# Four mixer steps traced later, and the branch sum moved from GpSimd to VectorE, in a hybrid decoder layer

## The chip, the cores and the metric

The kernel runs on one core of a Trainium2 chip. A core has TensorE (PE: matrix multiplies, with weight loads listed as PEld), VectorE (DVE), ScalarE (ACT), GpSimd (POOL) and SyncE (SP), each with an instruction queue that is worked off in order, and DMA engines that move data between HBM and the on-chip memories. The metric is the device time of one execution in microseconds. Before the change it is 2330.97 us, the median of three runs (2327.71, 2330.97 and 2331.9 us).

## The reference: what is computed

One layer on 256 tokens of width 2048, all float32. Cut to what matters:

```python
x = x + 0.5 * swiglu(rms_norm(x), ffn1...)            # d_ff 5632
h = rms_norm(x); p = h @ w_in                          # 1024 + 2*256 + 3360 + 4096 columns
q, k, v, p_rwkv, gates = split(p)
y_attn = sliding_window_attention(q, k, v, sinks)      # 16 heads of 64, 4 kv heads, blocks of 128
y_rwkv = rwkv7_time_mix(p_rwkv, ...)                   # recurrence over 256 steps, 16 heads of 64
gate_attn, gate_rwkv = split(sigmoid(gates))
merged = gate_attn * (y_attn @ w_proj_attn) + gate_rwkv * (y_rwkv @ w_proj_rwkv)
x = x + merged @ w_out
x = x + cross_attention(x, mem)
x = x + 0.5 * swiglu(rms_norm(x), ffn2...)
out = rms_norm(x)
```

The line `merged = ...` is the sum of the two branches. In the time mix, the decay and the rate `a` are sigmoids of small matrix products, and everything after them (keys, the inverse of a triangular system, the state) hangs on them.

## The kernel before, in words

**Products.** Nearly all TensorE time goes into products of the 256 tokens with weight matrices. A weight block arrives in units of 256 rows by up to 512 columns (`KU = 2` chunks of 128 rows). ScalarE rounds a unit to `hi` (line 299) and VectorE computes the rest `lo = raw - hi` (line 300). The activations are held as `hi` and `lo` too, and for each chunk and each half of the tokens `multiply` issues three matmuls of 512 columns: `xh*hi`, `xh*lo`, `xl*hi` (lines 336 to 338). These are called the large matmuls below; a unit has 12 of them. `next_unit` requests loads four units ahead on SP's queue and divides units two ahead (`LOADED`, `AHEAD`). `hi`, `lo` and `raw` have 3, 3 and 4 buffers. A product fills two PSUM banks (`acc`, of three); ScalarE or VectorE reads them at its end.

**Background steps.** Everything else in the mixer is written as Python generators, sorted into groups (`Interleave`). After each `multiply`, that is every six large matmuls, `tick` advances the first one, two or three generators of each group by one step, up to their next `yield`. So a `yield` places the following instructions six large matmuls later in the traced program; `idle(n)` is n yields. A planner that knows instruction costs then fixes each engine's final order, close to the traced order but not equal to it. On the chip each engine follows that order strictly: when an instruction's operand is late, all behind it on that engine wait.

**The steps the change touches**, in the order in which they run:
- `keys_values` (line 515): copies the keys into `kd` by ScalarE (line 521), mirrors them onto the other 64 partitions by two DMAs from GpSimd's queue (line 522), copies the values, idles, and then lets attention begin (`bg.seen.add("kv")`).
- `attend` (line 533), eight times, two at a time: scores (PE, line 542), scale and mask (DVE, line 548), row maximum (line 555), exponentials (ACT, line 567), normalization (DVE, lines 572 to 575), one yield, transposes of the probabilities (PE, line 581), copies (ACT, line 584), weighted values (PE, line 589).
- `decay_and_rate` (line 644): four groups of small matmuls (PE, line 661) into PSUM banks tagged `mm` (three of them, two per group), four sigmoids after each (ACT, line 668), one yield between the groups; then scans (DVE, line 675) and exponentials. It is the first of the serial group `ew`: `removal_keys` (lines 717 and 754), `substitute` (lines 775 to 789), `receptances` and `values` (lines 835 and 843) come behind it. The `pair` chains of the recurrence (lines 902 to 970) follow `values`, and `finish` (lines 995 to 1015) makes `yr` from them.
- the last part: four products of `yr` with `w_proj_rwkv`. At the end of each, VectorE multiplies by the gate (`gl`, line 1055), GpSimd adds the other branch (`ml`, line 1056), and `merged` transposes the sum on PE (line 347, tile `ml`) and splits it into `mt` (lines 352 and 353), which the product with `w_out` reads.

Of the kernel before, what the change touches and what calls it, by code (L numbers as in the profile page):

```python
# [120 lines left out]
def decoder_layer(ctx: ExitStack, tc: tile.TileContext, a: dict, out: bass.AP):  # L121
# [357 lines left out]
    with tc.tile_pool(name="mx", bufs=1, reuse_waits="tile") as sp:  # L479
# [35 lines left out]
        def keys_values():  # L515

            b = feat(tok_kv, C4[:2])
            v = kd[:].rearrange("p (c e) t -> p c e t", e=2)
            for e in range(2):
                r, o = slice(64 * e, 64 * e + 64), slice(64 - 64 * e, 128 - 64 * e)  # L520
                act.copy(v[r, :, e, :], b[r])
                pool.dma_start(v[o, :, e, :], v[r, :, e, :])
            yield
            for t in range(2):
                dve.tensor_copy(vt[:, t, :], tok_kv[:, t, KV_W : 2 * KV_W])
            yield from idle(2)
            bg.seen.add("kv")

        bg.spawn("feat", keys_values())
# [3 lines left out]
        def attend(kv, qb):  # L533
            yield from wait_for("kv")
            w = P * (qb + 1)
            tq = slice(qb * P, qb * P + P)
            s = t4("s", (P, 2, 2, T))
            b = [mm() for _ in range(2)]
            for c in range(2):
                for e in range(2):  # L540
                    r = slice(64 * e, 64 * e + 64)
                    pe.matmul(  # L542
                        b[e][:, c * w : (c + 1) * w], qt[kv // 2][r, 2 * (kv % 2) + c, tq],
                        kd[r, kv, :w], start=True, stop=True,
                    )
            bias = abias[:, 1 - qb :, :].rearrange("p a b -> p (a b)")
            for e in range(2):
                dve.scalar_tensor_tensor(
                    s[:, e, :, :w], b[e][:, : 2 * w].rearrange("p (c w) -> p c w", c=2), 0.125,
                    bias.unsqueeze(1).to_broadcast([P, 2, w]), ALU.mult, ALU.add,  # L550
                )
            yield
            s3 = s[:].rearrange("p e c w -> p (e c) w")
            m = stat.tile([P, 4], F32, tag="m", name="m")
            dve.tensor_reduce(m[:], s3[:, :, :w], AX.X, ALU.max)
            sk = sink4[:, kv]
            m22 = m[:].rearrange("p (e c) -> p e c", e=2)
            dve.tensor_tensor(m22, m22, sk, ALU.max)
            nm = stat.tile([P, 4], F32, tag="nm", name="nm")
            dve.tensor_scalar(nm[:], m[:], -1.0, None, ALU.mult)  # L560
            es = stat.tile([P, 4], F32, tag="es", name="es")
            dve.tensor_tensor(es[:].rearrange("p (e c) -> p e c", e=2), sk, m22, ALU.subtract)
            yield
            den = stat.tile([P, 4], F32, tag="den", name="den")
            act.activation(es[:], es[:], AF.Exp)
            for i in range(4):
                act.activation(
                    s3[:, i, :w], s3[:, i, :w], AF.Exp, bias=nm[:, i : i + 1],
                    accum_out=den[:, i : i + 1],
                )  # L570
            yield
            dve.tensor_tensor(den[:], den[:], es[:], ALU.add)
            dve.reciprocal(den[:], den[:])
            for i in range(4):
                dve.tensor_scalar(s3[:, i, :w], s3[:, i, :w], den[:, i : i + 1], None, ALU.mult)
            yield
            pt = t4("pt", (P, 2, 4, P))
            for kb in range(qb + 1):
                b = tr()
                for i in range(4):  # L580
                    pe.transpose(  # L581
                        b[:, i * P : (i + 1) * P], s3[:, i, kb * P : (kb + 1) * P], ident[:]
                    )
                act.copy(pt[:, kb], b[:].rearrange("p (i q) -> p i q", i=4))
            yield
            b = tr()
            for kb in range(qb + 1):
                for e in range(2):
                    pe.matmul(  # L589
                        b[64 * e : 64 * e + 64, : 2 * P], vt[:, kb, kv * 64 : kv * 64 + 64],  # L590
                        pt[:, kb, 2 * e : 2 * e + 2, :].rearrange("p c q -> p (c q)"),
                        start=kb == 0, stop=kb == qb,
                    )
            b3 = b[:, : 2 * P].rearrange("p (c q) -> p c q", c=2)
            hi, lo = (ya.at(p, 2 * kv, 2)[:, :, tq] for p in range(2))
            act.copy(hi, b3)
            dve.tensor_tensor(lo, b3, f32(hi), ALU.subtract)
            if qb:
                ya.done |= {2 * kv, 2 * kv + 1}
            if kv == 3 and qb:  # L600
                bg.seen.add("attn")
# [42 lines left out]
        def decay_and_rate():  # L644
            yield from wait_for("small")
            yield from wait_for("attn")
            wa = t4("wa", (P, RW))
            pool.dma_start(wa[0:64, :], W["rwkv_w2"])
            pool.dma_start(wa[64:128, :], W["rwkv_a2"])
            act.activation(xwa[0:64, :], xwa[0:64, :], AF.Tanh)  # L650
            act.activation(xg, xg, AF.Sigmoid)
            yield
            for h in range(2):
                cs.append(t4("cs"))
                aa.append(t4("aa"))
                for q in (0, 2):
                    b = [mm() for _ in range(2)]
                    for i in range(2):
                        for e in range(2):
                            r, c = slice(64 * e, 64 * e + 64), (4 * h + q + i) * P  # L660
                            pe.matmul(
                                b[e][:, i * T : (i + 1) * T], wa[r, c : c + P], xwa[r, :],
                                start=True, stop=True,
                            )
                    for i in range(2):
                        for e, (dst, bias) in enumerate(((cs[h], w0), (aa[h], a0))):
                            c = 4 * h + q + i
                            act.activation(
                                dst[:, q + i, :], b[e][:, i * T : (i + 1) * T], AF.Sigmoid,
                                bias=bias[:, c : c + 1],  # L670
                            )
                    yield
            for h in range(2):
                for c in range(4):
                    dve.tensor_tensor_scan(
                        cs[h][:, c, :], keep2, cs[h][:, c, :], 0.0, ALU.mult, ALU.add
                    )
                    if c % 2:
                        yield
                c3 = halves(cs[h])  # L680
                mid = stat.tile([P, 8], F32, tag="mid", name="mid")
                dve.tensor_copy(mid[:], c3[:, :, 63])
                dve.tensor_tensor(
                    c3, c3, mid[:].unsqueeze(2).to_broadcast([P, 8, P]), ALU.subtract
                )
                dec.append(stat.tile([P, 4], F32, tag="dec", name="dec"))
                dve.tensor_tensor(dec[h][:], cs[h][:, :, 127], mid[:, 1:8:2], ALU.add)
                yield
                act.activation(dec[h][:], dec[h][:], AF.Exp, scale=-DECAY)

                ee.append(t4("ee", (P, 8, P)))
                e0.append(stat.tile([P, 8], F32, tag="e0", name="e0"))
                act.activation(e0[h][:], mid[:], AF.Exp, scale=DECAY)
                act.activation(ee[h][:], c3, AF.Exp, scale=-DECAY)
                yield
                act.activation(cs[h][:], cs[h][:], AF.Exp, scale=DECAY)
                yield
            bg.seen.add("decay")
# [342 lines left out]
        mt = act_tiles("mt", 4)  # L1041

        def merged(m, n):
            yield
            for q in (0, 2):
                split(mt, 4 * n + q, 2, feat(m, C4[q : q + 2]))
                yield

        for n in range(4):
            g, m = t4("gl", (P, 2, 512)), t4("ml", (P, 2, 512))  # L1050
            pool.dma_start(g[:], blk(grd, n))
            pool.dma_start(m[:], blk(md, n))
            pr = product(yr, W["w_proj_rwkv"])
            for t in range(2):
                dve.tensor_tensor(g[:, t, :], pr[t][:], g[:, t, :], ALU.mult)
                pool.tensor_tensor(m[:, t, :], g[:, t, :], m[:, t, :], ALU.add)  # L1056
            bg.spawn("feat", merged(m, n))

        n3 = Norm(g_cross)
# [164 lines left out]
```

## Time and profile before

| | before |
|---|---|
| median of 3 runs | 2330.97 us (2327.71 to 2331.9) |
| the profiled execution | 2332.38 us, span 2330.7 us, mean granted TensorE clock 0.998 |
| PE busy | 2307.1 us (99%) |
| DVE, ACT, POOL busy | 1258.9 us (54%), 1078.9 us (46%), 130.3 us (6%) |
| HBM traffic | 185 GB/s over the span |
| the mixer's products | from about 748 us to about 1490 us of the span |

In the profile, times are counted from the span's start. A timeline row gives start, duration, engine, line, operation, tiles and shape, and how many instructions it merges; square brackets give the idle time of that engine just before, and what ended it. In a row of waits stand the total waited, how often, and the longest. PE is busy nearly all the time, so a change in another engine's work matters only where PE waits for that engine, or where the granted clock changes.

### The profile page before, as it was taken

To read this page: it belongs to the slowest core of one execution; us is meant where nothing else is said; L and a number is where in the kernel's file an instruction comes from. 1 tells how busy PE (TensorE), PEld (TensorE's weight loads), DVE (VectorE), ACT (ScalarE), POOL (GpSimd) and SP (SyncE) were. 2 spreads that over 40 slices of the span, in tenths; PEclk is the share of its full clock that TensorE was granted. 3 is DMA by queue.
4 is the path that set the end of the run, shared out by engine and by line. 5 is a ranking of instruction groups with operands and counts; after the bars stand their busy time and mean duration, and the time that the engine had idled before them with its cause. 6 is when DMAs were issued, how large, how long until landed. Compare 5 with 4: busy or idle time off the path is not lost.

```text
span 2330.7 us, 27378 instructions
## 1 busy us (share of the span) xinstructions
PE 2307.1 (99%) x10869; PEld 1898.4 (81%) x10869; DVE 1258.9 (54%) x1395; ACT 1078.9 (46%) x1425; POOL 130.3 (6%) x192
## 2 busy tenths in 40 slices
PE   8999999999999999999999999999999999999998
PEld 6888888888888877888888878888888888888887
DVE  4545544544556477795444556546545544544545
ACT  5443344434445477444344446555444344434444
POOL 1000000000000000200220030001000000000001
PEclk9999999999999999999999999999999999999999
DMA  8555655555554544666432576548555555555553
GB/s 284 187 189 191 197 184 197 182 198 192 187 188 153 172 129 140 196 229 212 123 96 94 165 247 216 201 158 298 187 192 187 193 196 184 198 182 197 191 189 127
DMA packets 219857, 432.71 MB, mean 186 GB/s; under 512 B 14268, under 2 KB 17041, under 8 KB 219729
## 3 DMA queue, kind: packets, MB, share of 16 engines
q1 hardware_dynamic: 211520, 405.58, 52.5%
q0 software_dynamic: 8176, 25.38, 3.4%
q8 instruction: 85, 1.39, 0.2%
q14 instruction: 44, 0.35, 0.0%
q10 hardware_dynamic: 32, 0.01, 0.0%
HBM read 417.56 MB, written 13.11 MB: 185 GB/s over the span
## 4 chain that ended last, share of the span: by engine, by line
PE 93%; issue 4%; DVE 1%; ACT 1%; POOL 1%; DMA 0%; SPq 0%; POOLq 0%; ACTq 0%
PE acc L336 28%; PE acc L337 28%; PE acc L338 28%; PE tr L347 2%; PE mm L934 1%; PE tr L902 1%; POOL ml L1056 0%; PE mm L542 0%; ACT hi L299 0%; PE tr L917 0%; DMA x<-in_x_dram 0%; PE tr L921 0%; PE tr L581 0%; PE tr L1004 0%; PE tr L589 0%
## 5 line engine op out<-in xcount | busy, mean ns | idle before, releaser
L300 DVE TENSOR_TENSOR lo<-raw,hi 128x1024 fp32r<-128x1024 f32 (+1 forms) x769 | 941.8, 1225 | 962.2 <-ACT hi L299 961.7
L299 ACT CAST hi<-raw 128x1024 fp32r<-128x1024 f32 (+1 forms) x769 | 805.6, 1048 | 1063.8 <-PE acc L338 1026.5
L336 PE MATMUL acc<-hi,xhi 128*128 128x512 f32 (+1 forms) x2016 | 799.2, 397 | 0.0
L337 PE MATMUL acc<-lo,xhi 128*128 128x512 f32 (+1 forms) x2016 | 786.0, 390 | 0.0
L338 PE MATMUL acc<-hi,xlo 128*128 128x512 f32 (+1 forms) x2016 | 785.4, 390 | 0.0
L336 PEld LDWEIGHTS acc<-hi,xhi 128*128 128x128 f32 x2016 | 379.9, 188 | 79.9 <-issue 3.6
L338 PEld LDWEIGHTS acc<-hi,xlo 128*128 128x128 f32 x2016 | 379.4, 188 | 79.8 <-issue 1.3
L337 PEld LDWEIGHTS acc<-lo,xhi 128*128 128x128 f32 x2016 | 380.0, 188 | 78.1 <-issue 3.3
L336 PE MATMUL acc<-hi,hhi 128*128 128x512 f32 x704 | 275.5, 391 | 0.0
L338 PE MATMUL acc<-hi,hlo 128*128 128x512 f32 x704 | 274.2, 389 | 0.0
L337 PE MATMUL acc<-lo,hhi 128*128 128x512 f32 x704 | 274.0, 389 | 0.0
L338 PEld LDWEIGHTS acc<-hi,hlo 128*128 128x128 f32 x704 | 132.1, 188 | 27.6
L337 PEld LDWEIGHTS acc<-lo,hhi 128*128 128x128 f32 x704 | 132.2, 188 | 27.1
L336 PEld LDWEIGHTS acc<-hi,hhi 128*128 128x128 f32 x704 | 132.2, 188 | 26.9
L336 PE MATMUL acc<-hi,mthi 128*128 128x512 f32 x128 | 51.2, 400 | 0.0
L338 PE MATMUL acc<-hi,mtlo 128*128 128x512 f32 x128 | 50.2, 392 | 0.0
L337 PE MATMUL acc<-lo,mthi 128*128 128x512 f32 x128 | 49.9, 390 | 0.0
L1177 POOL TENSOR_TENSOR x<-x,fin 128x512 f32<-128x512 f32 x6 | 8.9, 1507 | 695.3 <-ACT junk L1175 695.3
L470 POOL DMA_DIRECT2D x1d<-x x4 | 3.0, 745 | 710.4 <-DVE x L427 710.4
L415 ACT ACTIVATE hb<-acc,rs 128x512 f32<-128x512 f32 x44 | 30.2, 690 | 19.5 <-PE acc L338 19.5
L352 ACT CAST hhi<-tr 128x512 fp32r<-128x512 f32 x44 | 25.7, 584 | 16.3 <-PE tr L347 16.3
L373 ACT ACTIVATE xhi<-tr,gains 128x256 fp32r<-128x256 f32 x48 | 22.0, 471 | 22.0 <-DVE xlo L374 16.1
(289 smaller groups left out, 1641.3 us busy)
## 6 DMA issues: line engine op xcount, KB each, us to landing
raw<-in_ffn_w_up_dram SPq DMA_DIRECT2D x88, 1024.0 KB, 5.1
raw<-in_ffn_w_down_dram SPq DMA_DIRECT2D x88, 1024.0 KB, 5.0
raw<-in_ffn_w_gate_dram SPq DMA_DIRECT2D x86, 1024.0 KB, 5.1
raw<-in_w_in_dram SPq DMA_DIRECT2D x136, 512.0 KB, 3.5
raw<-in_w_out_dram SPq DMA_DIRECT2D x32, 512.0 KB, 4.3
raw<-in_w_proj_attn_dram SPq DMA_DIRECT2D x16, 512.0 KB, 3.7
raw<-in_w_proj_rwkv_dram SPq DMA_DIRECT2D x16, 512.0 KB, 5.0
raw<-in_w_cross_kv_dram SPq DMA_DIRECT2D x16, 512.0 KB, 3.5
```

What stands on the lines that cost most here:

```text
L299: act.copy(hi[:, s], raw[:, s])
L300: dve.tensor_tensor(lo[:, s], raw[:, s], f32(hi[:, s]), ALU.subtract)
L336: pe.matmul(o, xh, hi[:, i, :], start=k + i == 0, stop=False)
L337: pe.matmul(o, xh, lo[:, i, :], start=False, stop=False)
L338: pe.matmul(o, xl, hi[:, i, :], start=False, stop=k + i == nk - 1)
L347: pe.transpose(b[:, o : o + P], tok[:, t, col : col + P], ident[:])
L352: act.copy(x.at(0, c, n), src)
L373: last = act.activation(self.x.at(0, c), b[:, j, :], AF.Copy, scale=g)
L415: act.activation(hb[:, t, :], pg[t][:], AF.Silu, scale=norm.r[t])
L902: pe.matmul(b[e][:, m * P : (m + 1) * P], x1[r, j, cs_], x2[r, j, cs_], start=True, stop=True,)
L934: pe.matmul(vb[:, (o + e) * P : (o + e + 1) * P], lhs(e), rhs[:], start=first and e == 0, stop=True, **ek,)
L1177: pool.tensor_tensor(xs, xs, fin[:, n * 512 : (n + 1) * 512], ALU.mult)
```

## The change

Four background steps get more yields, and one addition changes its engine:

```diff
@@ keys_values
-            yield from idle(2)
+            yield from idle(4)
             bg.seen.add("kv")
@@ attend, between normalization and transposes
-            yield
+            yield from idle(2)
             pt = t4("pt", (P, 2, 4, P))
@@ decay_and_rate, after each of the four groups of sigmoids
-                    yield
+                    yield from idle(2)
@@ merged
         def merged(m, n):
-            yield
+            yield from idle(4)
@@ after each product of yr with w_proj_rwkv
                 dve.tensor_tensor(g[:, t, :], pr[t][:], g[:, t, :], ALU.mult)
-                pool.tensor_tensor(m[:, t, :], g[:, t, :], m[:, t, :], ALU.add)
+                dve.tensor_tensor(m[:, t, :], g[:, t, :], m[:, t, :], ALU.add)
```

Attention starts two ticks later and each attend takes one tick more; each decay group comes one tick later than it did; the transposes of the summed branches come three ticks later. No instruction is added to the program text, and none is removed. As the planner orders the changed program, ScalarE gets two more loads of an activation table.

## The prediction

> **What bounds the kernel now.** I read the page's busy shares and the chain that ended last, then PE's own waits, then the stretches and moments around those waits.
>
> ```profile
> PE 2307.1 (99%) x10869; PEld 1898.4 (81%) x10869; DVE 1258.9 (54%) x1395; ACT 1078.9 (46%) x1425; POOL 130.3 (6%) x192
> PE 93%; issue 4%; DVE 1%; ACT 1%; POOL 1%; DMA 0%; SPq 0%; POOLq 0%; ACTq 0%
> ```
>
> PE is the bound: 99% busy and 93% of the chain. The change removes no PE work, so only two things can move the time: moments at which PE waits for another engine, and the clock it is granted. PE's waits in the mixer:
>
> ```profile
> PE tr L347 <- POOL ml L1056: 3.1, 3, 1.0
> PE mm L542 <- DMA kd<-kd: 1.1, 1, 1.1
> PE tr L581 <- DVE s L575: 0.6, 1, 0.6
> PE mm L661 <- ACT aa L668: 0.5, 1, 0.5
> PE mm L661 <- ACT cs L668: 0.3, 1, 0.3
> ```
>
> Columns: total us, times, longest. These five rows add up to 5.6 us, and they are just the places where the change puts yields. That is most of what moving steps can win; the rest is the clock.
>
> **1. The branch sum.** The second of the four products of yr, from its end at 1367.6:
>
> ```profile
> 1367.32 1.28 DVE L1055 TENSOR_TENSOR gl<-acc,gl 128x512 f32<-128x512 f32 x2
> 1368.10 3.50 POOL L1056 TENSOR_TENSOR ml<-gl,ml 128x512 f32<-128x512 f32 x2 [8.20 <-DVE gl L1055]
> 1368.90 1.57 DVE L300 TENSOR_TENSOR lo<-raw,hi 128x1024 fp32r<-128x1024 f32 x1 [0.30 <-ACT hi L299]
> 1370.34 0.27 PE L347 MATMUL tr<-ident,ml 128*128 128x128 f32 x1
> 1371.65 0.55 PE L347 MATMUL tr<-ident,ml 128*128 128x128 f32 x3 [1.04 <-POOL ml L1056]
> ```
>
> PE transposes the first half, then waits for GpSimd's second addition. The stages, from one product's end to the next; the first row is the first product, which has no transposes of `ml`:
>
> ```profile
> 1344.60:1355.50 10.90, 10.90 (x50) 9.02 (x49) 5.12 (x5) 4.79 (x5) 2.14 (x3) 1.00 0.87 264
> 1355.50:1367.60 12.10, 12.03 (x57) 9.73 (x56) 7.88 (x9) 5.28 (x6) 3.93 (x4) 1.00 0.90 319
> 1367.60:1380.70 13.10, 12.05 (x58) 9.75 (x56) 7.84 (x9) 5.38 (x6) 4.89 (x4) 1.00 0.73 247
> 1380.70:1393.80 13.10, 12.06 (x58) 9.77 (x57) 7.85 (x9) 5.38 (x6) 4.17 (x3) 1.00 0.64 210
> ```
>
> Columns: length, then busy time of PE, PEld, DVE, ACT and POOL (instructions), clock, DMA share, GB/s. 48 large matmuls in 10.9 us make 0.227 us each. The two 13.1 us stages are 1.0 us longer than the 12.1 us one, where the additions came earlier; the fourth sum's transposes have the third 1.0 us wait. In the 12.1 us stage PE still loses some 0.2 us, so a stage without any wait is about 11.9 us and the four waits are worth 0.2 + 3 x 1.2 = 3.8 us.
>
> In the changed order the transposes stand 30 large matmuls behind the product in place of 12: 30 x 0.227 = 6.8 us. VectorE's order is `gl`, `gl`, `ml`, `ml`. The nearest row for an addition on VectorE with both operands in SBUF:
>
> ```profile
> L1008 DVE TENSOR_TENSOR yq<-yq,sq 128x512 f32<-128x512 f32 x4 | 2.7, 680 | 0.0
> L1056 POOL TENSOR_TENSOR ml<-gl,ml x8: 1278/1288/2243, 1356.0 to 1395.5; 128x512 f32<-128x512 f32 x8
> ```
>
> Two `gl` end 1.0 us after the product, two `ml` of 0.68 us each at 2.4 us: 4.4 us ahead of the transposes. The wait goes whole. The cost: VectorE gets 8 x 0.68 = 5.4 us. In each stage it goes from 7.85 of 13.1 to 9.2 of 11.9 us (77%), and the `lo` queued behind the additions, which took 1.57 us beside GpSimd, comes about 1.1 us later. That is hidden by the two units (24 x 0.227 = 5.4 us) that divisions run ahead; were that cover gone, four products would pay 1.1 to 1.4 us each. GpSimd's next `gl` and `ml` loads no longer queue behind the additions and can only start earlier. Term: -3.8, between -3.0 (the waits row) and -4.7 (with some contention saved).
>
> **2. The keys.**
>
> ```profile
> 816.54 0.29 PE L336 MATMUL acc<-hi,xhi 128*128 128x288 f32 x1
> 816.67 0.29 PE L337 MATMUL acc<-lo,xhi 128*128 128x288 f32 x1
> 818.94 0.64 POOL L522 DMA_DIRECT2D kd<-kd  x1 [62.87 <-ACT kd L521]
> 820.35 0.71 PE L542 MATMUL mm<-kd,qt 64*128 64x128 f32 x4
> 821.49 0.30 PE L336 MATMUL acc<-hi,xhi 128*128 128x288 f32 x1
> 822.89 1.57 PE L542 MATMUL mm<-kd,qt 64*128 64x128 f32 x12 [1.11 <-DMA kd<-kd]
> ```
>
> The mirrored keys land 3.9 us after their DMA is issued. Here a tick is short: matmuls of 288 columns start every 0.13 us, so two more ticks, 12 matmuls, are 1.6 us. PE reaches the scores at about 820.35 + 1.6 = 821.9 us; the first of them read no mirrored keys, the next ones wait until about 822.9. Some 0.5 of the 1.1 us goes. The DMAs themselves do not move. Term: -0.5, between 0 and -1.1.
>
> **3. Attention.** One more tick before the transposes is 1.36 us, against a wait of 0.6 us. But all eight attends move, and the planner's ScalarE order changes with them: the sigmoid of `xs`, with its two table loads, stood ahead of the fourth pair's exponentials and now stands ahead of the third's.
>
> ```profile
> 856.44 0.43 PE L581 MATMUL tr<-ident,s 128*128 128x128 f32 x2 [0.62 <-DVE s L575]
> 863.11 1.28 ACT L651 ACT_TABLE_LOAD   x1
> ```
>
> A table load takes 1.28 us. The third pair's normalization is what PE waited for, so the tick won may be used up by the loads. Term: 0, between -0.6 and +1.3 (one load exposed).
>
> **4. The decay groups.**
>
> ```profile
> 884.45 2.22 PE L661 MATMUL mm<-xs,wa 64*128 64x256 f32 x12 [0.25 <-ACT cs L668]
> 887.22 1.13 PE L661 MATMUL mm<-xs,wa 64*128 64x256 f32 x4 [0.55 <-ACT aa L668]
> ```
>
> PE waited 0.8 us because a group needs two of three `mm` banks and ScalarE had not emptied them. Before, six large matmuls lie between the first and the last of the four groups; in the changed order 25 do (6, 7 and 12). But the planner now slips an exponential between the second and third group's sigmoids: two more table loads, 2 x 1.28 us, behind which those sigmoids, a rounding and the fourth group's banks queue. Twelve large matmuls, 2.7 us, stand ahead of the fourth group as cover. Term: 0, between -0.8 and +2.6 (both loads exposed).
>
> **5. The clock.** PE does not only wait:
>
> ```profile
> 855.60:859.00 3.40, 2.78 (x14) 1.52 (x12) 3.29 (x13) 2.64 (x5) 1.17 (x3) 1.00 0.84 259
> 859.00:862.40 3.40, 3.40 (x14) 2.18 (x13) 1.60 (x2) 1.70 (x4) 0.00 (x0) 0.50 0.74 208
> 886.30:889.70 3.40, 2.85 (x11) 1.52 (x9) 3.33 (x7) 3.40 (x10) 0.00 (x0) 1.00 0.00 0
> 889.70:893.10 3.40, 3.40 (x9) 2.58 (x9) 3.30 (x7) 3.08 (x6) 0.00 (x0) 0.51 0.47 154
> ```
>
> Twice the granted clock is 0.5 for 3.4 us, each time behind 3.4 us in which PE was 0.55 to 0.62 us short and did almost no large matmul. Half a clock for 3.4 us costs 1.7 us. With 25 large matmuls among the decay groups the second should go; the first stands behind an attention pair that is as crowded as before, and may stay. Term: -1.7, between 0 and -3.4, or +1.7 if another thin stretch arises.
>
> The Trainium skill weighs against this term. "TensorE: Matmul & The Clock Gate", section "HAM oscillation — how this bites in real kernels", gives the rule as no idle gap over about 3.4 us; PE's longest wait here is 1.1 us, so by it the halved stretches are not due to these waits and the term is 0. The trace shows halved stretches without such a gap, so I keep the term.
>
> **6. What moves along.** Attention and the decay put the serial group `ew` ten ticks later: keys, inverse and values stand 60 large matmuls later (13.6 us), and so does the first step of the chains. GpSimd's `ld`, `xd`, `xb` and `g2` transfers and SP's four `dl` loads move with them.
>
> ```profile
> SPq L775 <- DMA ld<-lt: 4.9, 1, 4.9
> 1000.00:1040.00 40.00, 40.00 (x178) 33.11 (x177) 38.70 (x54) 16.53 (x17) 0.73 (x1) 1.00 0.66 215
> 1160.00:1200.00 40.00, 40.00 (x263) 33.96 (x263) 16.31 (x20) 17.63 (x40) 4.54 (x7) 1.00 0.19 56
> ```
>
> SP waits 4.9 us at `dl` with the weight loads queued behind it, before as after; loads run four units (10.9 us) ahead. In the substitution VectorE is 97% busy without PE waiting; it now ends just ahead of the receptances. The chains' last step stands 18 large matmuls later, still 102 (23 us) ahead of the product that reads yr. Term: 0; it would cost only what exceeds 23 us.
>
> **Sum.** -3.8 - 0.5 + 0 + 0 - 1.7 + 0 = -6.0 us, against the profiled execution's own 2332.38 us, which lies 1.4 us over the median of 2330.97. On the median: **2325.0 us** (0.26% less). All best ends: -4.7 - 1.1 - 0.6 - 0.8 - 3.4 = -10.6, 2320.4 us. All worst: -3.0 + 1.3 + 2.6 + 1.7 = +2.6, 2333.6 us.
>
> **Rivals.**
> - *The waits come back elsewhere.* Terms 3 and 4 go to their bad ends (+1.3, +2.6) and the clock stays: -3.8 - 0.5 + 3.9 = -0.4, 2330.6 us; half of it, 2328.6. For it: the table loads land on the engine PE waits for. Against: the covers above.
> - *The clock stays as it is.* -4.3 us, 2326.7 us: the case by the page's rule, on the edge of what counts as a change.
> - *The chains get too dense (slower).* Between their first and last steps stood 354 large matmuls, now 312, while the latencies of PE to ScalarE and back are the same. The 16 chain halves have some 8 ticks each. If each of these 128 lost 0.13 us, it would cost 16.6 us: 2331 - 6 + 16.6 = 2341.6 us. It decides from 0.05 us per tick, where the gain is gone. Against: in the stretch from 1160 to 1200, with three chains at once, PE is busy 40.00 of 40.00 us.
> - *It does nothing*: PE's order is in-order and the transposes demonstrably move, so I give this no chance of its own.
>
> **How the numbers follow.** The runs before spread over 4.2 us, and 0.2% (4.7 us) is about what a measurement of this kernel tells from no change. The forecast, with a gain over 4.7 us, gets 0.66; the kept clock 0.10, split between faster and same; the returned waits 0.16, same; the dense chains 0.08, slower. So faster 0.71, same 0.21, slower 0.08. The range goes from 2319 (the best ends and the runs' spread) to 2331.5 (the returned waits), and leaves out the dense chains and little else.
>
> **What would show it.** Right: PE's wait for `ml` is gone and the three stages are alike at about 11.9 us; the wait for `kd` is 0.4 to 0.7 us; one stretch of half clock at most. Wrong: a wait of L661 on L668 over 1.2 us, or of L581 on L575 over 0.6; a `lo` that PE waits for at the end of a product of yr; waits in the chains (L917, L934, L960) above the 0.2 us they have now; new half-clock stretches.

## The result and the profile after

The changed kernel is slower: 2339.4 us in the median (2336.94 to 2342.16), against 2329.89 us (2327.55 to 2333.53) for the kernel before, run beside it on the same chip. The ratio is 1.0043, 95% interval 1.0034 to 1.0052. The profiled execution took 2339.01 us, its span is 2337.2 us (before: 2332.38 and 2330.7).

The busy shares after:

```profile
PE 2312.1 (99%) x10869; PEld 1898.1 (81%) x10869; DVE 1261.3 (54%) x1403; ACT 1080.8 (46%) x1427; POOL 117.0 (5%) x184
```

PE is still the bound, with 5.0 us more busy time for the same 10869 matmuls. PE's waits after (total us, times, longest), without those at the program's start:

```profile
PE acc L336 <- ACT hi L299: 2.7, 1, 2.7
PE acc L337 <- DVE lo L300: 2.2, 4, 0.8
PE acc L336 <- DVE gl L1055: 2.1, 1, 2.1
PE acc L336 <- DVE ga L807: 0.8, 2, 0.6
PE mm L542 <- DMA kd<-kd: 0.7, 1, 0.7
...
PE tr L581 <- DVE s L575: 0.2, 1, 0.2
```

The waits that the change aimed at are gone from the list (`ml`, L661) or smaller (`kd` 1.1 to 0.7, L581 0.6 to 0.2). In their place stand three new rows, for rounded weights (`hi`, `lo`) and for the end of a product (`gl`), and one for `ga`.

The profiles are compared here by the number of large matmuls that PE has started, which is the same in every kernel. Where the 6.5 us between the two spans lie (worked out from the start times of the large matmuls):

```
large matmuls   what runs there                         before   after   difference
to the first    start of the program                      10.6     9.0    -1.6
0-3168          first FFN                                737.8   737.8     0.0
3456-4320       attention, decay, keys, inverse          239.8   238.1    -1.7
4320-5088       recurrence chains                        288.2   288.7    +0.5
5136-5280       last three products of yr                 38.3    41.6    +3.3
5280-5664       w_out                                     96.2    94.8    -1.4
6048-6240       first products of the second FFN          44.5    51.9    +7.4
6240-9216       rest of the second FFN                   693.8   693.8     0.0
```

The 1.6 us at the start are not the change's: in the 13 other profiles the first large matmul comes at 8.9 to 9.6 us, and only in that of the kernel before at 10.6.

The gain that the change aimed at is there: products of yr, first and third of these stages, are 11.8 us, and `w_out` wins its 1.4. Two places give more back than that. They are shown in the windows view (length, then busy time of PE, PEld, DVE, ACT, POOL with instructions, clock, DMA share, GB/s); after, the last three products of yr and the first products of the second FFN:

```profile
1352.68:1364.52 11.84, 11.84 (x58) 9.79 (x56) 4.90 (x7) 3.44 (x4) 0.70 (x1) 1.00 1.03 386
1364.52:1382.52 18.00, 15.31 (x58) 11.73 (x57) 12.00 (x15) 6.89 (x9) 0.72 (x1) 0.81 0.66 236
1382.52:1394.35 11.83, 11.83 (x58) 9.80 (x56) 8.50 (x11) 5.29 (x6) 0.72 (x1) 1.00 0.59 194
1591.49:1619.90 28.41, 25.21 (x105) 19.45 (x103) 10.87 (x17) 11.71 (x21) 6.51 (x10) 0.94 0.78 271
```

The third product of yr (the "second" in the expectations below) takes 18.00 us, 2.7 of them idle and a part at a lower clock, straight after a stage in which the DMA engines were saturated (share 1.03, 386 GB/s). The second FFN's first 96 large matmuls take 28.41 us; before they took 22.74:

```profile
1592.34:1615.08 22.74, 22.74 (x105) 18.76 (x104) 13.39 (x18) 13.94 (x22) 6.54 (x10) 1.00 0.87 304
```

**The first place: a burst of loads.** GpSimd's timeline after (start, duration, operation; "DMA_DIRECT2D" is the issue of a transfer):

```profile
1342.99 0.71 POOL L1038 DMA_DIRECT2D grd<-gr  x1 [19.61 <-ACT gr L1037]
1343.69 0.72 POOL L1051 DMA_DIRECT2D gl<-grd  x1
1344.41 0.70 POOL L1052 DMA_DIRECT2D ml<-md  x1
...
1348.59 0.72 POOL L1051 DMA_DIRECT2D gl<-grd  x1 [2.07 <-DMA grd<-gr]
1349.30 0.70 POOL L1052 DMA_DIRECT2D ml<-md  x1
1349.99 0.72 POOL L1073 DMA_DIRECT2D x<-x1d  x1
```

And the same queue before:

```profile
1347.21 0.72 POOL L1052 DMA_DIRECT2D ml<-md  x1
1355.97 2.53 POOL L1056 TENSOR_TENSOR ml<-gl,ml 128x512 f32<-128x512 f32 x2 [8.04 <-DVE gl L1055]
1358.45 0.72 POOL L1051 DMA_DIRECT2D gl<-grd  x1
...
1371.54 0.72 POOL L1051 DMA_DIRECT2D gl<-grd  x1
```

Before, the third and the fourth pair of `gl` and `ml` loads (1358.45 and 1371.54) each stood behind an addition on GpSimd's queue, and the addition waited for a product's end: from the second pair on, one pair per product, 12 to 13 us apart. The additions were a brake on the loads. After, no addition stands between the loads, and eight transfers of 512 KB are issued within 7.7 us, against the weight loads. What follows is in the rows of ScalarE, PE and VectorE after, and in the windows around the slow stretch:

```profile
1355.44 1.05 ACT L299 CAST hi<-raw 128x1024 fp32r<-128x1024 f32 x1 [4.23 <-DMA raw<-in_w_proj_rwkv_dram]
...
1359.30 1.05 ACT L299 CAST hi<-raw 128x1024 fp32r<-128x1024 f32 x1 [2.80 <-DMA raw<-in_w_proj_rwkv_dram]
...
1363.18 1.05 ACT L299 CAST hi<-raw 128x1024 fp32r<-128x1024 f32 x1 [2.84 <-DMA raw<-in_w_proj_rwkv_dram]
...
1365.55 0.50 PE L337 MATMUL acc<-lo,yrhi 128*128 128x512 f32 x1 [0.64 <-DVE lo L300]
...
1366.55 1.23 DVE L300 TENSOR_TENSOR lo<-raw,hi 128x1024 fp32r<-128x1024 f32 x1 [0.46 <-ACT hi L299]
...
1368.29 1.28 DVE L1055 TENSOR_TENSOR gl<-acc,gl 128x512 f32<-128x512 f32 x2
...
1369.03 0.80 PE L336 MATMUL acc<-hi,yrhi 128*128 128x512 f32 x1 [2.05 <-DVE gl L1055]
```

```profile
1365.00:1368.40 3.40, 1.43 (x5) 0.86 (x5) 2.94 (x5) 2.48 (x3) 0.00 (x0) 0.99 0.98 366
1368.40:1371.80 3.40, 2.77 (x7) 2.20 (x8) 3.40 (x5) 0.00 (x0) 0.72 (x1) 0.50 0.56 207
1371.80:1375.20 3.40, 3.40 (x10) 2.63 (x9) 1.33 (x2) 1.04 (x1) 0.00 (x0) 0.50 0.70 226
```

ScalarE, which should divide two units ahead, waits four times for weights (10.6 us in all; the three long ones are shown), so the lead is used up. `lo` comes late, the two gate products queue behind the late `lo`s on VectorE, PE's banks stay full (2.05 us), and PE is busy for only 1.43 of 3.40 us. Then the granted clock is 0.5 for 6.8 us, which costs some 3.4 us more.

**The second place: a tile at another address.** SyncE's weight loads for the second FFN after (one row for five issues: start of the first, time to the end of the last), and PE's row behind them:

```profile
1578.07 22.73 SPq L287 DMA_DIRECT2D raw<-in_ffn_w_gate_dram  x5
...
1606.16 0.73 PE L336 MATMUL acc<-hi,xhi 128*128 128x512 f32 x2 [2.67 <-ACT hi L299]
```

and before:

```profile
1578.92 7.86 SPq L287 DMA_DIRECT2D raw<-in_ffn_w_gate_dram  x5
1600.79 3.67 SPq L287 DMA_DIRECT2D raw<-in_ffn_w_up_dram  x3
```

Before, five `w_gate` loads were issued within 7.86 us; after, the last two of the five were issued only at about 1600, 22 us behind the first, and PE then waited 2.67 us for a rounded weight. These two are the first of the wide loads (tile `raw2`, 1 MB each), whose buffers lie where the mixer's tiles lay. The last residual tile `x2` must have been written out (`x3d<-x`) before its memory is overwritten. The tile allocator hands the mixer's slots out in the order in which tiles come free, and that order follows the traced program. The addresses that it gave (bytes per partition):

```
                  last x2 tile         first raw2          second raw2         third raw2
before            180192..184288       159712..167904      184288..192480      176096..184288
after             163808..167904       159712..167904      184288..192480      176096..184288
```

Before, the tile lies under the third wide load, and that one waits for the write, with two wide loads already issued. After, it lies under the first. SyncE's wait for the write is about as long in both (11.7 us before, 11.5 after); what changed is how many weight loads stand behind it.

### The profile page after: what moved, and what is told of

Read it like the earlier page. It is cut to its first block, busy times and chain, and to the rows that moved or that the text cites. A ratio compares the mean times of both kernels' runs of the same rounds, so it can differ in the third digit from the quotient of the medians.

```text
span 2337.2 us, 27381 instructions
## 1 busy us (share of the span) xinstructions
PE 2312.1 (99%) x10869; PEld 1898.1 (81%) x10869; DVE 1261.3 (54%) x1403; ACT 1080.8 (46%) x1427; POOL 117.0 (5%) x184
## 5 line engine op out<-in xcount | busy, mean ns | idle before, releaser
L373 ACT ACTIVATE xhi<-tr,gains 128x256 fp32r<-128x256 f32 x48 | 22.0, 471 | 21.8 <-DVE xlo L374 16.1
```

The lines of the kernel that those rows point to most:

```text
L373: last = act.activation(self.x.at(0, c), b[:, j, :], AF.Copy, scale=g)
```

## The experiments

My theory after the result: the loss is the burst (term 1's unpriced half) and the address (nowhere in my sum), and both are separate from the steps' delays as such. The rivals: VectorE's added load delays `lo` by itself; the denser chains; the later steps lose by themselves.

### Each half of the change alone

`add_only` changes the one line of the addition; `yields_only` has the four yields and leaves the addition on GpSimd.

> The kernel before with only the additions moved to VectorE; no yields. Theory A (the loss is in two side effects: GpSimd's queue, no longer held by the additions, issues its loads in one burst that starves the weight loads of the yr products; and the yields shift which memory the x2 tiles get, so that the second FFN's first weight load waits for the x3d write): here only the burst remains. The second product of yr takes 15 to 18 us in place of 13.1, the others 11.8 to 12.1, a half clock stretch near 1370 us, the second FFN starts as before; about 2332 us, between 2329 and 2335. Theory B (the yields alone cost the time, by denser background work in the mixer): 2326 us, since the waits on the GpSimd additions are gone and nothing is lost. Theory C (VectorE is overloaded by the additions): PE waits for lo or gl in all four yr products, some 1.5 us each; 2333 to 2336 us.

> The changed kernel with the additions back on GpSimd: only the four yields. Theory A: no burst, all yr products at 11.8 to 12.1 us since the transposes come 6.8 us after the product; the second FFN starts 7 us late as in the changed kernel; the mixer up to the yr products 1 us shorter; about 2332 us (2330 to 2334). Theory B: the mixer itself loses; 2338 to 2340 us. Theory C: no VectorE overload, 2326 us.

`add_only` took 2331.56 us (ratio 1.0009, 1.0000 to 1.0018), `yields_only` 2333.51 us (1.0020, 1.0010 to 1.0030). In `add_only` the third product of yr (large matmuls 5184 to 5232) takes 16.4 us, with a wait of 2.7 us for `gl` and a halved clock, while the two products on either side are down from 12.1 and 13.1 to 11.8 us; the second FFN's first stages are as before (22.7 and 21.8 us). In `yields_only` all three products are 11.8 us, and the second FFN's stages are 28.6 and 23.1 us. GpSimd's loads in `add_only` stand as close as in the changed kernel. So each accident belongs to one half: the burst to the addition, the address to the yields. In the products of yr the yields win alone what the whole change was to win there; moving the addition beside them adds nothing.

### The address

`after_hb` is the changed kernel with one tile tag declared earlier in the second FFN's pool, which shifts the `raw2` buffers upwards, away from the last `x2` tile. `yields_hb` does the same for `yields_only`.

```diff
     with tc.tile_pool(name="f2", bufs=1, reuse_waits="tile") as sp:
+        sp.tile([P, 2, 512], F32, tag="hb", name="hb", bufs=3)
         x = sp.tile([P, 2, D], F32, name="x")
```

> The changed kernel; in the second FFN's pool the hb buffers are laid out first, so that the weight buffer used first (raw2) no longer lies over the last x2 tile. Theory A: the second FFN's first wide load starts at once behind the narrow ones (about 1586 us, not 1600), the two products from large matmul 6048 on take 22.7 and 21.8 us as before and not 28.4 and 23.5; the burst stays; 2332 us (2330 to 2334), 7 us under the changed kernel. Theory B or C: the layout is without effect, 2339 us.

> The four yields, the additions on GpSimd, and hb laid out first: neither burst nor late first load. Theory A: the gains that the prediction counted remain: waits for ml gone (3.8 us), mixer 1 us shorter; 2325 us (2323 to 2327), faster than the kernel before by 0.2%. Theory B: 2337 us or more. Theory C: 2326 us.

`after_hb` took 2331.60 us (1.0012, 1.0003 to 1.0021), 7.8 us less than the changed kernel; `yields_hb` 2329.30 us (0.9993, 0.9984 to 1.0002), 4.2 us less than `yields_only`. In both, the stages at the second FFN's start are 22.7 and 21.8 us again; in `after_hb` the burst is still there, and the third product of yr takes 15.9 us. Theory A's 2325 us for `yields_hb` was missed by 4.3 us: without both accidents the yields still don't win what I had summed. (The profiled execution of `yields_only`, whose stages lose 7.2 us, was its longest, 2337.47 us; most of its other runs are some 4 us shorter, and no profile shows where.)

`before_bad` does the opposite: the kernel before, with a layout in which the first `raw2` buffer covers its last `x2` tile. No step of the mixer is moved.

```diff
-                hb = sp.tile([P, 2, 512], F32, tag="hb", name="hb", bufs=3)
+                hb = sp.tile([P, 2, 512], F32, tag="hb", name="hb", bufs=5)
@@ pool f2
+        sp.tile([P, 2, 512], F32, tag="hb", name="hb", bufs=5)
```

> The kernel before with nothing changed but the layout of the second FFN's pool: hb first and with five buffers, so that its first weight buffer lies over the last x2 tile, as in the changed kernel. If the place of that buffer alone makes the late start: the first wide load is issued near 1600 us and not near 1586, the two products from large matmul 6048 on take some 28 and 23 us in place of 22.7 and 21.8, and the time is 5 to 8 us over the kernel before, 2335 to 2338 us. If the late start comes from anything else in the changed order: 2330 us.

It took 2337.48 us (1.0031, 1.0020 to 1.0041), 7.6 us over the kernel before. SyncE's loads and PE's wait in the timeline of `before_bad`, and the stage in its windows:

```profile
1581.18 19.07 SPq L287 DMA_DIRECT2D raw<-in_ffn_w_gate_dram  x4
...
1605.47 0.73 PE L336 MATMUL acc<-hi,xhi 128*128 128x512 f32 x2 [2.58 <-ACT hi L299]
```

```profile
1590.88:1619.47 28.59, 24.03 (x106) 18.35 (x104) 10.87 (x17) 11.69 (x21) 6.53 (x10) 1.00 0.78 273
```

The last two of the four loads, again the first wide ones, come some 18 us behind the first, and PE's wait and the length of the stage are those of the changed kernel. The clock stayed at 1.00 here and was halved for 3.4 us in the changed kernel, yet the stages last the same: the halved clock cost nothing here, so the loads set the end. This accident is shown from both sides.

### The burst

`after_hb_brake` gives GpSimd a one-element addition (one element in each partition) behind each pair of additions, and its next loads, those of `x2` too, stay behind it. The additions themselves are on VectorE, as in the change.

```diff
+            with behind(n - 2):
                 pool.dma_start(g[:], blk(grd, n))
                 pool.dma_start(m[:], blk(md, n))
...
                 dve.tensor_tensor(m[:, t, :], g[:, t, :], m[:, t, :], ALU.add)
+            held.append(pool.tensor_tensor(tiny[:, n : n + 1], m[:, 1, 0:1], m[:, 1, 0:1], ALU.add))
```

> The changed kernel with hb laid out first, and with GpSimd's queue held again: behind each pair of additions GpSimd adds one column of ml (128x1), and the loads of gl and ml for the product after the next, and those of x2, are kept behind it, as they stood behind the additions before. VectorE does the same additions as in the changed kernel. If the burst of loads starves the weights: all yr products at 11.8 us, no wait of ScalarE on weights there, no half clock near 1370 us; about 5 to 7 us under after_hb, 2325 to 2329 us. If VectorE's load or the later lo is the cause: the second yr product stays at 16 to 18 us, 2332 us.

It took 2328.01 us (0.9988, 0.9980 to 0.9997), 3.6 us less than `after_hb` by the medians and 5.6 us by the two ratios. GpSimd's queue in the timeline of `after_hb_brake`, and in its windows the stage that was 18.00 us:

```profile
1355.08 0.19 POOL L1065 TENSOR_TENSOR tiny<-ml 128x1 f32<-128x1 f32 x1 [9.85 <-DVE ml L1063]
1355.57 0.73 POOL L1058 DMA_DIRECT2D gl<-grd  x1 [0.30 <-issue]
...
1367.03 1.10 POOL L1065 TENSOR_TENSOR tiny<-ml 128x1 f32<-128x1 f32 x1 [10.01 <-DVE ml L1063]
1368.06 0.72 POOL L1058 DMA_DIRECT2D gl<-grd  x1
```

```profile
1364.64:1376.48 11.84, 11.84 (x57) 9.80 (x56) 8.50 (x11) 5.29 (x6) 2.48 (x3) 1.00 0.77 269
```

PE is busy 11.84 of 11.84 us with the same additions on VectorE. The rival "VectorE's load delays `lo`" falls: what delayed `lo` was the weights.

`m_add_brake` has only the later transposes, the additions on VectorE and the brake.

> The later transposes of `merged` and the additions on VectorE, with a one-element GpSimd addition behind each pair that holds GpSimd's next loads back as the additions did before. Theory A (the additions on VectorE cost only through the loads that they no longer hold back, and win nothing once the transposes stand later): 2325.8 us within 1.5, no halved stretch in the products of yr and no wait for lo above 0.3 us there. Theory B (VectorE's 5.4 us more delays lo itself): waits for lo at the ends of the products, 0.5 us or more each, and 2327.5 us or more.

It took 2325.59 us (0.9982, 0.9973 to 0.9990), with 11.8 us for each of the three products. Among the transfers issued from 1340 to 1366 us (size, median time to landing) stand, after:

```profile
raw<-in_w_proj_rwkv_dram SPq DMA_DIRECT2D x8, 512.0 KB, 9.7
```

and in `m_add_brake`:

```profile
raw<-in_w_proj_rwkv_dram SPq DMA_DIRECT2D x9, 512.0 KB, 5.6
```

A weight load takes 9.7 us in the burst and 5.6 us without it. Loads run four units, 10.9 us, ahead of PE and ScalarE divides two units, 5.4 us, ahead, so a load has about 5.4 us to land without using up ScalarE's lead: 5.6 us is about that, 9.7 us is not.

### The yields one by one

`merged_only` is the kernel before with the later transposes alone (`idle(4)` in `merged`), additions on GpSimd.

> The kernel before with a single edit: the transposes of the branch sum three ticks later; the additions stay on GpSimd. No new burst, the same places in memory, the same attention and decay. The waits for ml go and nothing else changes: -3.8 to -4.0 us, 2326 us (2324.5 to 2327.5). If instead it is 2329 or more, the 3.8 us counted from the trace are not on the path.

It took 2325.79 us (0.9982, 0.9973 to 0.9991): 4.1 us less than before. Its three products take 11.8 us each in place of 12.1, 13.1 and 13.1, and `w_out` 95.2 in place of 96.2: 3.8 us in all. My term 1 was 3.8.

The other three yields were each added to it: the keys (`idle(4)`, and `idle(8)` in `merged_keys8`), attention, and the decay groups. In all of them the last `x2` tile lies away from the first wide load.

```diff
@@ m_keys4 (merged_keys8: idle(8))
-            yield from idle(2)
+            yield from idle(4)
@@ m_attend: attend; m_decay: decay_and_rate
-            yield
+            yield from idle(2)
```

> merged_only, and attention begins six ticks later than before (idle(8) in keys_values in place of 2; the change has 4). In six profiles the mirrored keys took 3.9 to 5.6 us to land, and PE's wait for them was 0.7 to 2.1 us whether they stood two ticks later or not, mostly with a stretch of half clock behind it. If their landing is what PE waits for, six ticks (about 5 us) cover it: no wait of L542 on kd, no half clock near 825 us, and 1 to 3 us less than merged_only, 2323 to 2325 us. Rival: the later attention pushes the substitution further against the gate products, and PE's wait for ga (0.8 us in the changed kernel) grows by as much; 2326 us or more.

> Only the later transposes of `merged` (which alone gave 2325.8 us) and the keys' two further ticks; additions on GpSimd, second FFN's buffers placed as before. Theory A (the mirrored keys land 3.9 to 5.6 us after their issue, whatever the order, so two ticks win less than the landing varies): PE's wait for kd stays between 0.7 and 2.1 us, a halved stretch follows it or not, and the time is 2325 to 2327.5 us. Theory B (the scores of both attends now queue at one place, and this costs more than the wait): waits of L581 or of lo come in addition and the time is above 2328 us. My prediction's term 2 would give 2325.3.

> Only the later transposes of `merged` and the one tick in attend. Theory A: L581's wait of 0.6 us goes, the wait for kd stays at 1.1 to 1.6, and the time is 2325 to 2326.5 us. Theory B (this yield is what costs the 2 to 3 us by which the four yields together lie above the later transposes alone): 2328 us or more, with a new wait between the keys and the decay. My prediction's term 3 would give 2325.2 to 2327.1.

> Only the later transposes of `merged` and the one tick in each decay group. Theory A: the waits of L661 (0.8 us) go and the halved stretch at 888 us (1.7 us) goes with them; in return VectorE's substitution, ten ticks of six large matmuls later, meets the gate product and PE waits for ga (0.8 us, two waits; stretch 1.0 us longer). Net -0.5 to -1.5: 2324.3 to 2325.5 us. Theory B (the collision with the gate product costs more than its own waits show): 2327 us or more, with the loss between large matmuls 3744 and 4320.

| beside `merged_only` (2325.79) | us | ratio to before, interval |
|---|---|---|
| keys, two ticks (`m_keys4`) | 2339.41 | 1.0034, 1.0021 to 1.0046 |
| keys, six ticks (`merged_keys8`) | 2328.16 | 0.9993, 0.9984 to 1.0002 |
| attention, one tick (`m_attend`) | 2327.52 | 0.9987, 0.9979 to 0.9996 |
| decay groups, one tick each (`m_decay`) | 2325.33 | 0.9978, 0.9969 to 0.9987 |
| all three, `yields_hb` | 2329.30 | 0.9993, 0.9984 to 1.0002 |

None of the three wins anything that can be measured, and the keys' two ticks alone lose 13.6 us (five runs). `merged_keys8` fits neither of its theories: the wait for `kd` and the halved stretch behind it are gone, yet the time is 2.4 us above `merged_only`, and no wait for `ga` is there.

For `m_keys4`, theory A fell and theory B has a part of the reason. The `kd` wait is 2.1 us, and there are waits of 1.6 us for the normalization (L581) and 1.4 us for `tok`, as theory B has it. PE's rows at the attention pair in the timeline of `m_keys4`, and two of its windows:

```profile
849.63 0.92 PE L581 MATMUL tr<-ident,s 128*128 128x128 f32 x4 [0.35 <-DVE s L575]
851.77 1.97 PE L581 MATMUL tr<-ident,s 128*128 128x128 f32 x8 [1.23 <-DVE s L575]
855.10 0.48 PE L347 MATMUL tr<-ident,tok 128*128 128x128 f32 x1 [1.35 <-ACT tok L494]
```

```profile
850.80:854.20 3.40, 1.97 (x8) 1.57 (x8) 3.18 (x10) 1.22 (x5) 0.00 (x0) 0.63 0.00 0
854.20:857.60 3.40, 2.50 (x7) 1.20 (x8) 0.49 (x3) 1.35 (x4) 0.00 (x0) 0.50 0.00 0
```

PE waits 2.9 us here within 6 us, and the granted clock is 0.5 for 6.8 us; `merged_only` waits 0.6 us at this place, at full clock. The largest single wait, though, is at the decay groups, which the edit doesn't touch and neither theory has. ScalarE's rows and then PE's in the timeline of `m_keys4`, and two of its windows:

```profile
898.33 1.28 ACT L693 ACT_TABLE_LOAD   x1
...
899.85 1.28 ACT L668 ACT_TABLE_LOAD   x1
901.15 0.47 ACT L668 ACTIVATE cs<-mm,rv 128x256 f32<-128x256 f32 x1
...
902.40 1.61 PE L661 MATMUL mm<-xs,wa 64*128 64x256 f32 x4 [2.91 <-ACT cs L668]
```

```profile
898.40:901.80 3.40, 1.09 (x5) 0.63 (x4) 1.63 (x4) 3.36 (x5) 0.00 (x0) 1.00 0.00 0
901.80:905.20 3.40, 2.80 (x8) 1.89 (x9) 2.13 (x4) 3.16 (x8) 0.00 (x0) 0.66 0.02 5
```

In this order the planner puts a small exponential between the sigmoids of the second and the third decay group, with two table loads of 1.28 us. The sigmoids behind them are late, no large matmul stands between the groups, and PE waits 2.91 us for the last group's banks; then it is granted less clock. (`merged_only` waits 0.8 us at its decay groups, and a halved stretch of 3.4 us stands behind them too.) That is the bad end of my term 4 (2.6 us, both loads exposed), in a kernel without the decay yields. In the changed kernel the same exponential stands between the same groups:

```profile
894.39 1.28 ACT L693 ACT_TABLE_LOAD   x1
...
895.91 1.28 ACT L668 ACT_TABLE_LOAD   x1
```

There PE has no wait at L661 in its list, and large matmuls stand between the groups. So the yields aren't additive: with attention's and the decay's added (`yields_hb`), 10.1 of the 13.6 us come back; its list has 0.2 us for L581 and nothing for L661. Which of the two yields clears which place is not shown: the keys' yield was not run with only one of them. `m_attend` came in between its two theories; it lost the wait at L581 and got one of 1.7 us for `lo` and one of 1.4 us in the chains.

`m_decay` came in within theory A's time but not by theory A's route: the `ga` wait didn't appear, a wait of 1.4 us in the chains (L917 for `mk`) and a halved stretch at 858 us did, and the `L661` waits fell from 0.8 to 0.3 us. The stretch from 3744 to 4320 is 2.1 us longer, which is where theory B had put a loss. The `ga` wait (0.8 to 0.9 us) is there in the changed kernel, `yields_only`, `after_hb`, `yields_hb` and `after_hb_brake`, where all three are together.

## Why the prediction was wrong

I forecast 2325.0 us and faster; it is 2339.4 us and slower. On the medians the step from 2329.9 to 2339.4 is 9.5 us; taking the address away gives 7.8 back, and holding the loads back another 3.6. Without the two, the change as a whole gives 2328.0 us, 1.9 us less than before, against the 6.0 I summed. The miss of 14.4 us is thus 7.8 for the address, 3.6 for the burst and 4.1 for steps that won less than I gave them, less the 1.1 us by which the kernel before measured lower beside the changed one than in the three runs I started from (2329.9 against 2331.0). Each of these sizes is good to some 2 us, as the intervals of the ratios are.

- **Term 1, the branch sum (-3.8): right in size, wrong in two steps.** The wait for `ml` goes and the stages are alike at 11.8 us; `merged_only` measured 3.8 us for it in the stages and 4.1 us in the medians. But either half alone wins it (the products next to the burst are 11.8 us in `add_only` too), so the engine's change was not needed, and the sentence "GpSimd's next `gl` and `ml` loads no longer queue behind the additions and can only start earlier" was the failure. I had the mechanism in hand and counted earlier as harmless. It cost 3.6 us by the medians; in the three profiles that have the burst, the product behind it is 4.1 to 6.2 us longer. The sign I listed for it under "wrong", a `lo` that PE waits for at the end of a product of yr, is in the trace (0.64 us, and 2.05 us for `gl` behind it). The numbers were there: a DMA share of 0.87 to 0.90 in the windows I had quoted for the first two products, and GpSimd's pairs of loads, 1 MB each, which the additions kept a product apart. The cost that I did price, VectorE's, came out small: its busy time per product is 8.50 us with the additions (`after_hb_brake`) and not 9.2, since `lo` takes 1.23 us there, not the 1.57 us that it took beside GpSimd's addition.
- **Term 6, "what moves along" (0): incomplete.** I followed the transfers and the chains, and not the memory. A step moved in the traced order changes the order in which tiles are taken and freed, and so their addresses; one tile came to lie under the second FFN's first wide load. 7.6 to 7.8 us, shown both ways (4.2 us by the medians of `yields_only` and `yields_hb`). It was the larger half of the miss, and no rival of mine named it (the dense chains' 2341.6 us lies near the result, by a mechanism that the runs don't show). The chains themselves did what I wrote: 288.2 became 288.7 us.
- **Term 2, the keys (-0.5): the size can't be had.** I took 3.9 us for the landing of the mirrored keys from one row. Over the profiles it lies between 3.8 and 5.6 us, and PE's wait for it between 0.7 and 2.1 us, with the same order: 0.7 in the changed kernel, 2.1 in `yields_only`. Two more ticks are 1.6 us. Six more (`merged_keys8`) take the wait away, and waits of 1.9 us (L581) and 1.0 us (`lo`) come in its place.
- **Term 3, attention (0): not refuted**: `m_attend` is 1.7 us above `merged_only`, and their intervals overlap.
- **Term 4, the decay groups (0): right here.** L661's waits are gone from the list, and the two table loads are covered as I wrote. `m_keys4` shows the cost I named when the cover is gone: 2.91 us.
- **Term 5, the clock (-1.7): given back.** The stretches at 859 and 889.7 us are gone, 3.4 us of halved clock each. New ones of 6.8 and 3.4 us stand at 1368 and 1607 us, behind the two accidents. In `add_only`, `yields_only`, `after_hb`, `yields_hb`, `merged_only`, `m_keys4` and `m_add_brake` a halved stretch at 822 to 825 us follows the wait for `kd` (1.2 to 2.1 us); in `before_bad`, `m_attend` and `m_decay` none follows waits of 1.3 to 1.6 us. The Trainium skill, page "TensorE: Matmul & The Clock Gate", section "HAM oscillation — how this bites in real kernels", asks for a gap over about 3.4 us. Here PE's longest wait before a halved stretch is 2.05 us (1368) and 2.67 us (1607), so the trace speaks against a single long gap as the condition. A low share of busy time in 3.4 us isn't enough either: PE was busy 0.73 of 3.40 us just ahead of the stretch at 1607, and 0.73 of 3.40 us from 1602.9 on in `before_bad`, where the clock stayed at 1.00. What sets the halved clock is open.
- **The rivals.** The dense chains fell (+0.5 us, not +16.6). Waits did come back elsewhere, but not at the decay and attention, where I had put them. The kept clock (2326.7 us) had the mean clock about unchanged, which it is (0.998 and 0.996), and misses the time for the same two reasons as my forecast.

What stays open: how the landing time of `kd` spreads over the runs of one kernel, since each kernel has one profile; and with it how much of the 2.2 us between `merged_only` and `after_hb_brake` is lost to the `ga` wait (its stretch, large matmuls 3744 to 4320, is 1.0 us longer) and how much to the keys' wait and the clock behind it.

The best kernels of the study, `m_decay`, `m_add_brake` and `merged_only` (2325.3 to 2325.8 us), can't be told apart; each beats both kernels, and the edit that they share is the transposes that stand three ticks later.

## What to carry to other kernels

An instruction that waits on an in-order queue may be the only thing that spaces out the transfers behind it: before moving it to another engine, list the transfers that it held back, their bytes, and how much of the DMA engines the weight loads leave. Moving steps in a traced program also moves tiles: compare the addresses of the tiles that the next stage's first loads overwrite, because there a late write holds up the whole load queue. And measure the edits of a bundle one by one and together: here one edit of five carried the gain, and one of the others cost 13.6 us beside it, of which the rest gave 10.1 back.

## What was unexpected of the hardware

- The same mirroring DMA of the keys, at the same place in the order, landed between 3.8 and 5.6 us after its issue from one kernel's profile to the next.
- A 512 KB weight load took 9.7 us in place of 5.6 us when eight other 512 KB transfers had been issued from GpSimd's queue within 7.7 us; the DMA engines moved 386 GB/s in that stage.
- A clock of 0.5 followed 3.4 us in which PE was busy 1.43 us (1368) or 0.73 us (1607), with no single wait above 2.7 us; in `before_bad` PE was also busy only 0.73 of 3.40 us at the same place, no such stretch followed, and the stage took as long.
